# Average pooling over 671 MB: every transfer issued by GpSimd on one queue, each as one packet per DMA engine

## The chip, the cores and the metric

The kernel runs on one core of a Trainium2 chip. The metric is the device time of one execution in microseconds (us); a kernel's time is the median of several runs. A transfer between the chip's memory (HBM) and the core's on-chip memory of 128 partitions is carried by 16 DMA engines; an engine of the core issues it, and the kernel's instructions wait for its completion by a semaphore.

## The reference

Means over windows of four neighbours, without overlap, of a float32 array of 64 x 256 x 8192 (536.87 MB in, 134.22 MB out):

```python
def reference(x, kernel_size, stride):          # 4 and 4
    batch, channels, length = x.shape           # 64, 256, 8192
    out_len = (length - kernel_size) // stride + 1
    output = np.zeros((batch, channels, out_len), dtype=np.float32)
    for i in range(out_len):
        start = i * stride
        output[:, :, i] = np.mean(x[:, :, start : start + kernel_size], axis=2)
    return output
```

## The kernel before

The array is seen as 16384 rows of 8192 numbers. `_packed_fast_path` (the path that this shape takes) cuts them into 32 groups of 512 rows; a partition holds four neighbouring rows of a group, f = 0 to 3. So a group is four input tiles `xt` of 128 x 8192 (4 MiB each, 32 KiB in each partition) and one output tile `ot` of 128 x 8192 (also 4 MiB).

For each tile the loop does three things: SyncE (SP) issues the load (L245); VectorE (DVE) adds the four neighbours with one `tensor_reduce` into a quarter of `ot` (L246); ScalarE (ACT) multiplies that quarter by 1/4 in place (L252). After the fourth tile, ACT issues the store of the whole group (L253). There are three buffers for `xt` and two for `ot`; a load into a buffer waits for the reduce that read it last. SP's queue thus holds the loads, ACT's queue the stores, and both queues run on the same 16 DMA engines.

The last group is cut finer, so that little is left to do after the last byte has arrived: its second and third tile are loaded and reduced in thirds (L263, L266), its fourth in six pieces of falling size (L284, L293), 1668, 2268, 1632, 1172, 844 and 608 columns. The first three tiles' results of this group (6144 columns) are stored by SP in four equal parts, issued behind the last piece's load (L292). The results of the first five pieces are stored by ACT, one by one (L310); the last piece is scaled by VectorE into a tile of its own, `fin` (L300), and stored by SP (L307).

On SP the order is: loads of all tiles, the four parts of the last group's store, the last piece's store. On ACT: four scalings, one store, and so on. GpSimd (POOL) only sets four constants.

Of the kernel before, what the change touches and what calls it, by code (L numbers as in the profile page):

```python
# [7 lines left out]
_N_PARK = 4  # L8
_FINAL_COLS_TGT = 608
_LADDER_RATIO = 1.39  # L10
_NCHUNK_PRE = 3
_PACK_STORES = True
_PACK_F_MAX = 4


def _tail_ladder(total: int, k: int, final: int, ratio: float = _LADDER_RATIO,
                 max_chunks: int = 12) -> list:
    if total < 4 * final:
        return [total]
    rev = []  # L20
    s = 0
    w = float(final)
    while len(rev) < max_chunks - 1:
        wi = max(k, (int(round(w)) // k) * k)
        if s + wi > total - k:
            break
        rev.append(wi)
        s += wi
        w *= ratio
    sizes = [total - s] + rev[::-1]  # L30
    assert sum(sizes) == total and all(x > 0 and x % k == 0 for x in sizes)
    return sizes


def _even_chunks(total: int, k: int, n: int) -> list:
    n = max(1, min(n, total // k))
    q = (total // n) // k * k
    sizes = [q] * n
    sizes[-1] += total - q * n
    assert sum(sizes) == total and all(s > 0 and s % k == 0 for s in sizes)  # L40
    return sizes


@with_exitstack
def kernel(
    ctx: ExitStack,
    tc: tile.TileContext,
    x: bass.AP,
    kernel_size: bass.AP,
    stride: bass.AP,  # L50
    out: bass.AP,
):
    nc = tc.nc

    K = int(kernel_size)
    S = int(stride)
    assert K == S, "only stride == kernel_size supported"

    B, C, L = x.shape
    OL = (L - K) // S + 1  # L60
    assert OL * K <= L

    P = nc.NUM_PARTITIONS

    xf = x.flatten_outer_dims()
    of = out.flatten_outer_dims()
    rows = B * C

    inv_k = 1.0 / float(K)
    dt = x.dtype  # L70
    IL = OL * K

    if _PACK_STORES and IL == L:
        F = 0
        for cand in range(_PACK_F_MAX, 1, -1):
            if rows % (P * cand) == 0 and (rows // (P * cand)) >= 2:
                F = cand
                break
        if F >= 2 and L >= 64 * K and OL % 8 == 0 and OL * F * 4 <= 32768:
            _packed_fast_path(nc, tc, xf, of, rows, L, OL, K, F, inv_k, dt, P)  # L80
            return

    RPP = 1
    R = P * RPP
    NT = rows // R
    IL2 = RPP * L
    OL2 = RPP * OL
    fast = (
        IL == L
        and rows % R == 0  # L90
        and NT >= 6
        and IL2 >= 64 * K
        and OL % 2 == 0
    )

    if not fast:
        with (
            tc.tile_pool(name="xin", bufs=4) as pin,
            tc.tile_pool(name="res", bufs=4) as pout,
        ):  # L100
            r0 = 0
            while r0 < rows:
                rn = min(P, rows - r0)
                xt = pin.tile([P, IL], dt)
                ot = pout.tile([P, OL], dt)
                nc.sync.dma_start(out=xt[:rn], in_=xf[r0 : r0 + rn, :IL])
                nc.vector.tensor_reduce(
                    out=ot[:rn],
                    in_=xt[:rn].rearrange("p (m k) -> p m k", k=K),
                    axis=mybir.AxisListType.X,  # L110
                    op=mybir.AluOpType.add,
                )
                nc.scalar.mul(ot[:rn], ot[:rn], inv_k)
                nc.scalar.dma_start(out=of[r0 : r0 + rn], in_=ot[:rn])
                r0 += P
        return

    def xview(t):
        return xf[t * R : (t + 1) * R]

    def oview(t):
        return of[t * R : (t + 1) * R]

    ladder = _tail_ladder(IL2, K, _FINAL_COLS_TGT)
    chunks_pre = _even_chunks(IL2, K, _NCHUNK_PRE)
    fin_w = ladder[-1] // K

    with (
        tc.tile_pool(name="xin", bufs=4) as pin,
        tc.tile_pool(name="res", bufs=4) as pout,  # L130
        tc.tile_pool(name="rsv", bufs=1) as prsv,
        tc.tile_pool(name="fin", bufs=1) as pfin,
    ):
        rsv = prsv.tile([P, OL2], dt)
        fin = pfin.tile([P, fin_w], dt)

        for t in range(NT):
            xv = xview(t)
            ov = oview(t)
            xt = pin.tile([P, IL2], dt)  # L140
            ot = rsv if t == 0 else pout.tile([P, OL2], dt)

            if t == 0:
                nc.sync.dma_start(out=xt[:, :IL2], in_=xv[:, :IL2])
                nc.vector.tensor_reduce(
                    out=ot[:, :OL2],
                    in_=xt[:, :IL2].rearrange("p (m k) -> p m k", k=K),
                    axis=mybir.AxisListType.X,
                    op=mybir.AluOpType.add,
                )  # L150
                nc.scalar.mul(ot[:, :OL2], ot[:, :OL2], inv_k)
            elif t < NT - 3:
                nc.sync.dma_start(out=xt[:, :IL2], in_=xv[:, :IL2])
                nc.vector.tensor_reduce(
                    out=ot[:, :OL2],
                    in_=xt[:, :IL2].rearrange("p (m k) -> p m k", k=K),
                    axis=mybir.AxisListType.X,
                    op=mybir.AluOpType.add,
                )
                nc.scalar.mul(ot[:, :OL2], ot[:, :OL2], inv_k)  # L160
                nc.scalar.dma_start(out=ov[:, :OL2], in_=ot[:, :OL2])
            elif t < NT - 1:
                c0 = 0
                for cw in chunks_pre:
                    c1 = c0 + cw
                    o0, o1 = c0 // K, c1 // K
                    nc.sync.dma_start(out=xt[:, c0:c1], in_=xv[:, c0:c1])
                    nc.vector.tensor_reduce(
                        out=ot[:, o0:o1],
                        in_=xt[:, c0:c1].rearrange("p (m k) -> p m k", k=K),  # L170
                        axis=mybir.AxisListType.X,
                        op=mybir.AluOpType.add,
                    )
                    nc.scalar.mul(ot[:, o0:o1], ot[:, o0:o1], inv_k)
                    nc.scalar.dma_start(out=ov[:, o0:o1], in_=ot[:, o0:o1])
                    c0 = c1
            else:
                nchunk = len(ladder)
                c0 = 0
                for i, cw in enumerate(ladder):  # L180
                    c1 = c0 + cw
                    o0, o1 = c0 // K, c1 // K
                    last = i == nchunk - 1
                    nc.sync.dma_start(out=xt[:, c0:c1], in_=xv[:, c0:c1])
                    if last:
                        q0 = 0
                        qw = (OL2 - q0) // _N_PARK
                        for qi in range(_N_PARK):
                            qa = q0 + qi * qw
                            qb = q0 + (qi + 1) * qw if qi != _N_PARK - 1 else OL2  # L190
                            nc.sync.dma_start(
                                out=oview(0)[:, qa:qb], in_=rsv[:, qa:qb]
                            )
                    nc.vector.tensor_reduce(
                        out=ot[:, o0:o1],
                        in_=xt[:, c0:c1].rearrange("p (m k) -> p m k", k=K),
                        axis=mybir.AxisListType.X,
                        op=mybir.AluOpType.add,
                    )
                    if last:  # L200
                        nc.vector.tensor_scalar(
                            out=fin[:, :fin_w],
                            in0=ot[:, o0:o1],
                            scalar1=inv_k,
                            scalar2=None,
                            op0=mybir.AluOpType.mult,
                        )
                        nc.sync.dma_start(out=ov[:, o0:o1], in_=fin[:, :fin_w])
                    else:
                        nc.scalar.mul(ot[:, o0:o1], ot[:, o0:o1], inv_k)  # L210
                        nc.scalar.dma_start(out=ov[:, o0:o1], in_=ot[:, o0:o1])
                    c0 = c1


def _packed_fast_path(nc, tc, xf, of, rows, L, OL, K, F, inv_k, dt, P):
    R = P * F
    NTM = rows // R

# [10 lines left out]
    with (  # L229
# [6 lines left out]
        for t in range(NTM):  # L236
            xv = xe(t)
# [109 lines left out]
```

## Time and profile before

| | |
|---|---|
| median of 3 runs | 1561.14 us (1561.12 to 1561.38) |
| profiled execution, first to last instruction | 1559.04 us |
| bytes read from HBM and written to it | 536.87 MB, 134.22 MB |
| mean rate over the span | 430 GB/s |
| one reduce of a whole tile (VectorE, L246) | 8686 ns, 124 of them |
| one scaling of 128 x 2048 (ScalarE, L252) | 1911 ns, 124 of them |
| one issue of a load by SP / of a store by ACT | 328 ns / 338 ns |
| a load's time from issue to landing, median | 26.4 us |
| a group store's time from issue to landing, median | 23.2 us |

How to read it: the span is one execution as the hardware profiler saw it. "Busy" counts only work of the engine itself; issuing a transfer does not count. A transfer's data move as packets on the 16 DMA engines; a packet record has a start, a duration, a size and a queue. Of a table by stretches of time the columns are: the stretch, its length, then busy time and number of instructions of VectorE, ScalarE and GpSimd, the clock granted to the (unused) TensorE, the mean busy share of the 16 DMA engines, and the bytes moved per time. The share can exceed 1 a little, since neighbouring packets of an engine overlap in the records.

### The profile page before, as it was taken

To read this page: it belongs to the slowest core of one execution; us is meant where nothing else is said; L and a number is where in the kernel's file an instruction comes from. 1 tells how busy PE (TensorE), PEld (TensorE's weight loads), DVE (VectorE), ACT (ScalarE), POOL (GpSimd) and SP (SyncE) were. 2 spreads that over 40 slices of the span, in tenths; PEclk is the share of its full clock that TensorE was granted. 3 is DMA by queue.
4 is the path that set the end of the run, shared out by engine and by line. 5 is a ranking of instruction groups with operands and counts; after the bars stand their busy time and mean duration, and the time that the engine had idled before them with its cause. 6 is when DMAs were issued, how large, how long until landed. Compare 5 with 4: busy or idle time off the path is not lost.

```text
span 1559.0 us, 724 instructions
## 1 busy us (share of the span) xinstructions
DVE 1112.8 (71%) x138; ACT 247.4 (16%) x137; POOL 0.2 (0%) x4
## 2 busy tenths in 40 slices
DVE  6777667776667866677666776667766677766786
ACT  1111111111111111111111111111111111111111
POOL 0000000000000000000000000000000000000000
DMA  9999999999999999999999999999999999999999
GB/s 416 418 430 436 437 432 430 430 430 432 439 433 430 430 432 430 438 434 431 430 432 430 435 434 433 431 431 430 433 437 433 432 430 431 430 437 434 432 427 384
DMA packets 25637, 671.14 MB, mean 430 GB/s; under 512 B 2848, under 2 KB 3488, under 8 KB 4768
## 3 DMA queue, kind: packets, MB, share of 16 engines
q1 hardware_dynamic: 20448, 540.10, 80.6%
q10 hardware_dynamic: 5184, 131.00, 19.5%
q14 instruction: 5, 0.04, 0.0%
HBM read 536.87 MB, written 134.22 MB: 430 GB/s over the span
## 4 chain that ended last, share of the span: by engine, by line
DMA 75%; DVE 24%; issue 0%; SPq 0%; DVEq 0%
DMA xt<-in_x_dram 75%; DVE ot L246 23%; DVE ot L293 1%; DVE ot L266 0%; SPq L263 0%; DVEq L246 0%; DVE fin L300 0%
## 5 line engine op out<-in xcount | busy, mean ns | idle before, releaser
L246 DVE TENSOR_REDUCE ot<-xt 128x2048 f32<-128x8192 f32 x124 | 1077.1, 8686 | 430.2 <-DMA xt<-in_x_dram 430.2
L252 ACT ACTIVATE ot<-ot 128x2048 f32<-128x2048 f32 x124 | 237.0, 1911 | 1270.2 <-DVE ot L246 1270.2
L266 DVE TENSOR_REDUCE ot<-xt 128x682 f32<-128x2728 f32 (+2 forms) x7 | 26.6, 3809 | 6.9 <-DMA xt<-in_x_dram 6.9
L272 ACT ACTIVATE ot<-ot 128x682 f32<-128x682 f32 (+2 forms) x7 | 6.6, 936 | 25.8 <-DVE ot L266 25.8
L293 DVE TENSOR_REDUCE ot<-xt 128x417 f32<-128x1668 f32 (+5 forms) x6 | 9.0, 1568 | 0.0
L309 ACT ACTIVATE ot<-ot 128x417 f32<-128x417 f32 (+4 forms) x5 | 2.6, 521 | 5.2 <-DVE ot L293 5.2
L252 ACT ACT_TABLE_LOAD x1 | 1.3, 1283 | 0.7 <-PEq L328 0.7
L300 DVE TENSOR_SCALAR fin<-ot 128x152 f32<-128x152 f32 x1 | 0.2, 239 | 0.0
L328 POOL MEMSET const-bfloat16-1.0<- 128x1 bf16 x1 | 0.1, 102 | 0.0
L328 POOL MEMSET const-uint8-127<- 128x1 uint8 x1 | 0.1, 102 | 0.0
L328 POOL MEMSET const-float32-0.0<- 128x1 f32 x1 | 0.1, 99 | 0.2 <-issue 0.2
L328 POOL MEMSET const-float32-1.0<- 128x1 f32 x1 | 0.1, 99 | 0.0
## 6 DMA issues: line engine op xcount, KB each, us to landing
xt<-in_x_dram SPq DMA_DIRECT2D x125, 4096.0 KB, 26.4
out_dram<-ot ACTq DMA_DIRECT2D x31, 4096.0 KB, 23.2
xt<-in_x_dram SPq DMA_DIRECT2D x4, 1364.0 KB, 23.4
out_dram<-ot SPq DMA_DIRECT2D x4, 768.0 KB, 7.7
xt<-in_x_dram SPq DMA_DIRECT2D x2, 1368.0 KB, 29.5
xt<-in_x_dram SPq DMA_DIRECT2D x1, 1134.0 KB, 16.2
xt<-in_x_dram SPq DMA_DIRECT2D x1, 834.0 KB, 22.6
xt<-in_x_dram SPq DMA_DIRECT2D x1, 816.0 KB, 17.8
```

The source lines that it names most:

```text
L246: nc.vector.tensor_reduce(out=ot[:, o0 : o0 + OL], in_=xt[:, :L].rearrange("p (m k) -> p m k", k=K), axis=mybir.AxisListType.X, op=mybir.A ...
L252: nc.scalar.mul(ot[:, o0 : o0 + OL], ot[:, o0 : o0 + OL], inv_k)
L266: nc.vector.tensor_reduce(out=ot[:, o0:o1], in_=xt[:, c0:c1].rearrange("p (m k) -> p m k", k=K), axis=mybir.AxisListType.X, op=mybir.AluOp ...
L272: nc.scalar.mul(ot[:, o0:o1], ot[:, o0:o1], inv_k)
L293: nc.vector.tensor_reduce(out=ot[:, o0:o1], in_=xt[:, c0:c1].rearrange("p (m k) -> p m k", k=K), axis=mybir.AxisListType.X, op=mybir.AluOp ...
L300: nc.vector.tensor_scalar(out=fin[:, :fin_w], in0=ot[:, o0:o1], scalar1=inv_k, scalar2=None, op0=mybir.AluOpType.mult,)
L309: nc.scalar.mul(ot[:, o0:o1], ot[:, o0:o1], inv_k)
L328: nc = _bacc.Bacc("TRN2", target_bir_lowering=False, num_devices=1)
```

## The change

The kernel is written anew around the same tiling: 32 groups, four tiles each, the same thirds and the same six pieces at the end. What differs:

- Every transfer, load and store, is issued by GpSimd (`dma = nc.gpsimd`), whose descriptors are written by software, and all stand in one queue in program order. SP and ACT issue none.
- Every transfer carries `single_packet=True`: each engine's share of a transfer is one packet.
- There are four buffers for `xt` in place of three.
- A group's store isn't issued after its last scaling, but behind the second load of the next group (`AHEAD = 2`).
- The end: all six pieces' loads, then the four parts of the store of the first three tiles (`PARK = 4`), then one store for the first four pieces and one for the last two. The last two pieces are scaled by VectorE in place; `fin` is gone.

```diff
-        tc.tile_pool(name="xin", bufs=3) as pin,
-        tc.tile_pool(name="res", bufs=2) as pout,
-        tc.tile_pool(name="fin", bufs=1) as pfin,
...
-                    nc.sync.dma_start(out=xt[:, :L], in_=xv[:, f * L : (f + 1) * L])
...
-                nc.scalar.dma_start(out=ov[:, : F * OL], in_=ot[:, : F * OL])
...
+    dma = nc.gpsimd
...
+    pin = ctx.enter_context(tc.tile_pool(name="xin", bufs=4))
+    pout = ctx.enter_context(tc.tile_pool(name="res", bufs=2))
+
+    def load(g, xt, f, a, b):
+        dma.dma_start(out=xt[:, a:b], in_=xg(g)[:, f * L + a : f * L + b], single_packet=True)
+
+    def means(xt, ot, f, a, b, scale_on_dve=False):
+        o = ot[:, f * OL + a // K : f * OL + b // K]
+        nc.vector.tensor_reduce(
+            out=o,
+            in_=xt[:, a:b].rearrange("p (m k) -> p m k", k=K),
+            axis=mybir.AxisListType.X,
+            op=mybir.AluOpType.add,
+        )
+        if scale_on_dve:
+            nc.vector.tensor_scalar(
+                out=o, in0=o, scalar1=1.0 / K, scalar2=None, op0=mybir.AluOpType.mult
+            )
+        else:
+            nc.scalar.mul(o, o, 1.0 / K)
+
+    def store(g, ot, a, b):
+        dma.dma_start(out=og(g)[:, a:b], in_=ot[:, a:b], single_packet=True)
+
+    held = None
+    for g in range(groups):
+        ot = pout.tile([P, F * OL], dt, name="ot")
+        for f in range(F):
+            xt = pin.tile([P, L], dt, name="xt")
+            if (g, f) == (groups - 1, F - 1):
+                break
+            cuts = THIRDS if g == groups - 1 and f > 0 else (L,)
+            edges = [sum(cuts[:i]) for i in range(len(cuts) + 1)]
+            for a, b in zip(edges[:-1], edges[1:]):
+                load(g, xt, f, a, b)
+            if held is not None and f == AHEAD - 1:
+                store(*held, 0, F * OL)
+            for a, b in zip(edges[:-1], edges[1:]):
+                means(xt, ot, f, a, b)
+        held = g, ot
+
+    f = F - 1
+    edges = [sum(LADDER[:i]) for i in range(len(LADDER) + 1)]
+    n = len(LADDER) - 2
+    for a, b in zip(edges[:-1], edges[1:]):
+        load(g, xt, f, a, b)
+    for i in range(PARK):
+        store(g, ot, i * f * OL // PARK, (i + 1) * f * OL // PARK)
+    for a, b in zip(edges[:n], edges[1 : n + 1]):
+        means(xt, ot, f, a, b)
+    store(g, ot, f * OL, f * OL + edges[n] // K)
+    for a, b in zip(edges[n:-1], edges[n + 1 :]):
+        means(xt, ot, f, a, b, scale_on_dve=True)
+    store(g, ot, f * OL + edges[n] // K, F * OL)
```

More of the change, by code (lines that the diff above doesn't have):

```diff
@@ L6 @@
 from concourse._compat import with_exitstack
[L8 to L41, printed above, removed]
+F = 4
+AHEAD = 2
+LADDER = (1668, 2268, 1632, 1172, 844, 608)
+THIRDS = (2728, 2728, 2736)
+PARK = 4
 @with_exitstack
@@ L53 @@
     nc = tc.nc
-    K = int(kernel_size)
-    S = int(stride)
-    assert K == S, "only stride == kernel_size supported"
+    K, S = int(kernel_size), int(stride)
+    assert K == S == 4
     B, C, L = x.shape
-    OL = (L - K) // S + 1
-    assert OL * K <= L
+    OL = L // K
     P = nc.NUM_PARTITIONS
+    dt = x.dtype
+    dma = nc.gpsimd
     xf = x.flatten_outer_dims()
     of = out.flatten_outer_dims()
[L67 to L77, printed above, removed]
-                break
-        if F >= 2 and L >= 64 * K and OL % 8 == 0 and OL * F * 4 <= 32768:
-            _packed_fast_path(nc, tc, xf, of, rows, L, OL, K, F, inv_k, dt, P)
-            return
@@ L83 @@
[L83 to L131, printed above, removed]
-        tc.tile_pool(name="fin", bufs=1) as pfin,
[L133 to L212, printed above, removed]
@@ L215, in _packed_fast_path @@
-def _packed_fast_path(nc, tc, xf, of, rows, L, OL, K, F, inv_k, dt, P):
-    R = P * F
-    NTM = rows // R
-    ladder = _tail_ladder(L, K, _FINAL_COLS_TGT)
-    chunks_pre = _even_chunks(L, K, _NCHUNK_PRE)
-    fin_w = ladder[-1] // K
-    def xe(t):
-        return xf[t * R : (t + 1) * R].rearrange("(p f) m -> p (f m)", f=F)
-    def oe(t):
-        return of[t * R : (t + 1) * R].rearrange("(p f) m -> p (f m)", f=F)
-    with (
-        tc.tile_pool(name="xin", bufs=3) as pin,
-        tc.tile_pool(name="res", bufs=2) as pout,
-        tc.tile_pool(name="fin", bufs=1) as pfin,
-    ):
-        fin = pfin.tile([P, fin_w], dt)
-        for t in range(NTM):
-            xv = xe(t)
-            ov = oe(t)
-            ot = pout.tile([P, F * OL], dt)
-            if t < NTM - 1:
-                for f in range(F):
-                    xt = pin.tile([P, L], dt)
-                    o0 = f * OL
-                    nc.sync.dma_start(out=xt[:, :L], in_=xv[:, f * L : (f + 1) * L])
-                    nc.vector.tensor_reduce(
-                        out=ot[:, o0 : o0 + OL],
-                        in_=xt[:, :L].rearrange("p (m k) -> p m k", k=K),
-                        axis=mybir.AxisListType.X,
-                        op=mybir.AluOpType.add,
-                    )
-                    nc.scalar.mul(ot[:, o0 : o0 + OL], ot[:, o0 : o0 + OL], inv_k)
-                nc.scalar.dma_start(out=ov[:, : F * OL], in_=ot[:, : F * OL])
-                continue
-            for f in range(F - 1):
-                xt = pin.tile([P, L], dt)
-                widths = [L] if f < F - 3 else chunks_pre
-                c0 = 0
-                for cw in widths:
-                    c1 = c0 + cw
-                    o0, o1 = f * OL + c0 // K, f * OL + c1 // K
-                    nc.sync.dma_start(
-                        out=xt[:, c0:c1], in_=xv[:, f * L + c0 : f * L + c1]
-                    )
-                    nc.vector.tensor_reduce(
-                        out=ot[:, o0:o1],
-                        in_=xt[:, c0:c1].rearrange("p (m k) -> p m k", k=K),
-                        axis=mybir.AxisListType.X,
-                        op=mybir.AluOpType.add,
-                    )
-                    nc.scalar.mul(ot[:, o0:o1], ot[:, o0:o1], inv_k)
-                    c0 = c1
-            fq = F - 1
-            xt = pin.tile([P, L], dt)
-            hold = fq * OL
-            nchunk = len(ladder)
-            c0 = 0
-            for i, cw in enumerate(ladder):
-                c1 = c0 + cw
-                o0, o1 = fq * OL + c0 // K, fq * OL + c1 // K
-                last = i == nchunk - 1
-                nc.sync.dma_start(
-                    out=xt[:, c0:c1], in_=xv[:, fq * L + c0 : fq * L + c1]
-                )
-                if last:
-                    qw = hold // _N_PARK
-                    for qi in range(_N_PARK):
-                        qa = qi * qw
-                        qb = (qi + 1) * qw if qi != _N_PARK - 1 else hold
-                        nc.sync.dma_start(out=ov[:, qa:qb], in_=ot[:, qa:qb])
-                nc.vector.tensor_reduce(
-                    out=ot[:, o0:o1],
-                    in_=xt[:, c0:c1].rearrange("p (m k) -> p m k", k=K),
-                    axis=mybir.AxisListType.X,
-                    op=mybir.AluOpType.add,
-                )
-                if last:
-                    nc.vector.tensor_scalar(
-                        out=fin[:, :fin_w],
-                        in0=ot[:, o0:o1],
-                        scalar1=inv_k,
-                        scalar2=None,
-                        op0=mybir.AluOpType.mult,
-                    )
-                    nc.sync.dma_start(out=ov[:, o0:o1], in_=fin[:, :fin_w])
-                else:
-                    nc.scalar.mul(ot[:, o0:o1], ot[:, o0:o1], inv_k)
-                    nc.scalar.dma_start(out=ov[:, o0:o1], in_=ot[:, o0:o1])
-                c0 = c1
@@ new lines, with xg, og @@
+    R = P * F
+    groups = B * C // R
+    assert B * C == groups * R
+    assert sum(LADDER) == sum(THIRDS) == L
+    def xg(g):
+        return xf[g * R : (g + 1) * R].rearrange("(p f) m -> p (f m)", f=F)
+    def og(g):
+        return of[g * R : (g + 1) * R].rearrange("(p f) m -> p (f m)", f=F)
+    pin = ctx.enter_context(tc.tile_pool(name="xin", bufs=4))
+    pout = ctx.enter_context(tc.tile_pool(name="res", bufs=2))
+    def load(g, xt, f, a, b):
+        dma.dma_start(out=xt[:, a:b], in_=xg(g)[:, f * L + a : f * L + b], single_packet=True)
```

## The prediction

> **What bounds the kernel now.** I read the page first, busy times, slices and queues; then the chain that ended last; then the answer by stretches of time; then the timeline of the end; last the trace's records of single packets.
>
> ```profile
> span 1559.0 us, 724 instructions
> DVE 1112.8 (71%) x138; ACT 247.4 (16%) x137; POOL 0.2 (0%) x4
> ...
> DMA packets 25637, 671.14 MB, mean 430 GB/s; under 512 B 2848, under 2 KB 3488, under 8 KB 4768
> q1 hardware_dynamic: 20448, 540.10, 80.6%
> q10 hardware_dynamic: 5184, 131.00, 19.5%
> ...
> DMA xt<-in_x_dram 75%; DVE ot L246 23%; DVE ot L293 1%; DVE ot L266 0%; SPq L263 0%; DVEq L246 0%; DVE fin L300 0%
> ```
>
> VectorE is busy for 71%, ScalarE for 16%, GpSimd for nothing. The two queues (q1 of SP, q10 of ACT) together hold the 16 DMA engines for 80.6 + 19.5 = 100.1% of the span. So the chain's 23% on L246 misleads: it goes through VectorE because a load waits for a buffer, but the DMA engines never lack work meanwhile. The stretches say so:
>
> ```profile
> 20.00:40.00 20.00, 17.97 (x3) 3.82 (x2) 0.00 (x0) 1.00 1.00 433
> ...
> 886.31:1031.76 145.45, 104.23 (x12) 22.93 (x12) 0.00 (x0) 1.00 1.00 433
> ...
> 1540.00:1550.00 10.00, 9.91 (x8) 3.38 (x6) 0.00 (x0) 1.00 1.02 413
> 1550.00:1559.00 9.00, 0.00 (x0) 0.00 (x0) 0.00 (x0) 1.00 0.68 268
> ```
>
> The last two columns are DMA share and GB/s. From 886.31 to 1031.76 us the chain passes exactly three groups (four loads and one store of 4 MiB each), 145.45 / 3 = 48.48 us a group, and the share is 1.00. The time is thus bytes over the engines' rate, plus a head and a tail. A change pays if it makes an engine spend less than 48.48 us on its 1,310,720 bytes of a group, or if it shortens the ends.
>
> **What an engine's time is made of.** The packet records have one packet for each 32 KiB row and one of 4 bytes for each completion: (128 + 16) x 142 transfers = 20448, q1's number. Median durations: 4 B 9 ns, 608 B 31 ns, 6144 B 234 ns, 32768 B 1213 ns. The slope of the last two is 979 / 26624 = 0.03677 ns a byte, so the bytes of a 32 KiB packet take 1204.9 ns, and about 8 ns are the packet's own, as for the packet of 4 bytes. A group's bytes need 1,310,720 x 0.03677 = 48.20 us; 48.48 - 48.20 = 0.28 us is overhead, 6.3 ns for each of its 45 packets (less than 8, since neighbours overlap).
>
> **The change, part by part.** *One packet for each engine and transfer.* Of a group's 45 packets an engine keeps 5. If all that overhead goes with the boundaries, 32 groups win 32 x 0.28 = 9 us; if it belongs to each row's descriptor, nothing is won. No row shows a packet of several rows. I take a part: large packets average 3.1 ns over their median, half of it in 52 stretched ones, so some 1.6 of the 6.3 ns is scatter that no boundary makes. The nearest row, the 4-byte packet, costs its 9 ns with next to no data, which speaks for the packet as the cause. So 4.7 ns x 40 x 32 = **-6.0 us** (0 to -9).
>
> The Trainium skill has a rule against this part. In "DMA: Bandwidth & Descriptors", section "Why small descriptors are slow (HBM only)", it gives a fixed overhead of about 3 cycles for a packet and holds that joining descriptors is only worth it up to 256 bytes each. With the 850 MHz of its section "Where 436 GB/s comes from" that would be an estimate of 3.5 ns x 40 x 32 = -4.5 us, and by its verdict on large descriptors 0.
>
> *Stores.* 174 transfers in place of 178: the end has two stores for its last 2048 columns, not six. 4 x 9 packets x 6.3 ns = -0.2 us.
>
> *The start.* Before, SP issues at 0.73 us and the first packet starts at 1.73 us. Now GpSimd writes the descriptors. No row has that; the bounds are 0 and the cost of code being loaded as in ACT_TABLE_LOAD, 1.28 us, taken twice, 2.6. I take +1.0. At 54 us, when the first store joins, ten packets of about 2 us stand in the records; the 5 us stretches from 50 and 55 us are about 16 and 68 GB/s short of 433, together 1.0 us. One queue and a fourth buffer may remove that: 0 to -1.0, taken -0.5.
>
> *One queue in order.* A store now stands between loads. Let a group's last load land at T. Its reduce takes 8.69 us and its scaling 1.91, so the store issues at T + 10.7. Behind it on GpSimd wait the third and fourth load of the next group, and VectorE waits for them. Ahead of it are two loads, 2 x 9.7 = 19.4 us of DMA work. The cover is 8.7 us, so nothing is lost; if it were gone, each us beyond it would cost 1 us in each of 31 groups. Loads wait for the reduce of the tile four before, which ends 8.7 us after that tile lands, with three loads still queued. A group's output buffer returns one group before it is wanted. Cost 0. The 31 store issues leave ACT (338 ns each, under 84% idle time) and 137 load issues leave SP: 0. GpSimd had four memsets, and 174 issues at any price below 1559 / 174 = 8.9 us fit.
>
> L246 takes 8686 ns for 8192 inputs, 1.06 ns each; if GpSimd could write no descriptor while a reduce runs, the store would be put off to the end of the reduce then running, T + 18.4, still inside 19.4, so even that costs about 0. A second rule of the Trainium skill is the reason to ask: "SBUF — State Buffer", section "SBUF: two separate sides", warns that VectorE in a two-port mode locks GpSimd out of writing descriptors. "VectorE: DVE Perf Modes" lists this reduce with a 1x form only, so by the pages no lock is due.
>
> *The tail.*
>
> ```profile
> 1540.65 9.02 DVE L293 TENSOR_REDUCE ot<-xt 128x417 f32<-128x1668 f32 x6
> ...
> 1549.71 0.24 DVE L300 TENSOR_SCALAR fin<-ot 128x152 f32<-128x152 f32 x1
> ...
> 1552.79 0.38 SPq L307 DMA_DIRECT2D out_dram<-fin x1
> ```
>
> The last store issues 2.8 us after its data are ready, yet packets run until 1556, the last one to 1557.6. The 1.6 us of ramp there is the most to win. After, 4 MiB of stores, 9.7 us, stand behind the last load, while reduce, two scalings and an issue need about 3 us: hidden. A slower GpSimd issue may cost as much: -1.5 to +1.5, taken 0.
>
> Sum: -6.0 - 0.2 + 1.0 - 0.5 + 0 = **-5.7 us**, on the span of 1559.04: 1553.3. The runs' median, 1561.14, lies 2.1 us above that span (work outside the first and last instruction); kept, this gives **1555.4 us**.
>
> **Rivals.** *A, the forecast*: the overhead belongs to packet boundaries. For it: 9 ns for 4 bytes. Against: a boundary and a descriptor are the same thing in every row.
>
> *B, nothing is joined, or joining doesn't pay*: the overhead is each row's. Then the sum is -0.2 + 1.0 - 0.5 = +0.3, 1561.4 us. For it: a large packet is within 0.7% of its pure bytes. It is also the case that the change doesn't do what it says.
>
> *C, slower: a gap at the head of each transfer on the one software-written queue*. The place is the hand-over from one transfer to the next on each engine: with one queue no other has packets ready to fill it. Price: g x 174. Against it, from 20 to 40 us only loads run, on one queue, at share 1.00: hardware-written transfers follow without a gap, so the lower bound is 0. The other bound is the 0.33 us that SP's issuing instruction takes for one transfer, if that were spent at every hand-over: 57 us, 1613. It decides from 5.7 / 174 = 33 ns on. Between ends so far apart I place C at 0.08 us, a quarter of the upper, since the one queue's row is near 0: +14 us, 1569.
>
> **How the numbers follow.** About 0.2% (3.1 us) is what a measurement can tell from no change: 1558.0 to 1564.3 is the same. A 0.57, B 0.18, C 0.25. Of A 0.53 is faster and 0.04 the same (a small packet gain with a dear start); of B 0.03, 0.11 and 0.04 are faster, same and slower; of C 0.01 is the same and 0.24 slower. Faster 0.56, same 0.16, slower 0.28. The low end takes A's bounds: -9 - 0.2 - 1.0 = -10.2 and half of the tail's gain, 1550. The high end is C's placed value, 1569; about half of C lies beyond, 0.12, and some 0.04 below the low end. A's own range is 1550 to 1559.
>
> **What would show it.** A: packets fall from 25637 towards a fifth or less or, if the records still list rows, these take less than 1213 ns; the group's period falls below 48.4 us, the middle slices rise from 433 to 434 to 435 GB/s. B: the period stays at 48.48. C: the share in the middle falls below 1.00, with idle stretches as often as there are transfers. Start: the first reduce, at 12.74 us before, comes about 1 us later. One queue: GpSimd's waits for ScalarE must not leave the DMA share under 1.00 in mid-group. The prediction falls if the rate of single packets changes (more than 0.03677 ns a byte), or if the first load lands many us late.

## The result, and the profile after

The changed kernel takes 1566.20 us (median of 6 runs, 1565.48 to 1566.45) against 1561.13 us before (6 runs, 1560.99 to 1561.40): slower by 5.07 us, ratio 1.0032 with a 95% interval of 1.0023 to 1.0042. The forecast was 1555.4 us, faster. The profiled execution took 1565.48 us, with a span of 1563.56 us.

The page of the changed kernel, its busy times, packet count and queue, then the chain that ended last:

```profile
span 1563.6 us, 685 instructions
DVE 1112.7 (71%) x139; ACT 246.8 (16%) x136; POOL 91.9 (6%) x178
...
DMA packets 24852, 671.13 MB, mean 429 GB/s; under 512 B 2784, under 2 KB 2784, under 8 KB 3984
q0 software_dynamic: 24848, 671.10, 99.8%
...
DMA xt<-in_x_dram 81%; DVE ot L58 17%; POOL xt L54 0%; POOLq L135 0%; POOL out_dram L72 0%; POOLq L72 0%; PEldq L135 0%
```

One queue, q0, carries everything, as the change says. But there are 24852 packets, not a fifth of 25637: hardly any were joined. That a transfer goes as one packet for each engine, as the title and the list of changes have it, isn't what the records show. The DMA engines are still the bound (99.8%). GpSimd spends 92 us on issuing, 6% of the span.

The stretches of the changed kernel, with the same columns as before:

```profile
886.31:1031.76 145.45, 104.16 (x13) 22.91 (x12) 7.89 (x15) 1.00 1.00 432
...
1550.00:1563.00 13.00, 2.47 (x5) 0.45 (x1) 1.07 (x2) 1.00 0.59 247
```

In the middle the share is 1.00, as before, and the rate hardly differs. So most of the 5 us must be sought at the two ends.

The start, from the timeline of the kernel before:

```profile
0.73 75.33 SPq L245 DMA_DIRECT2D xt<-in_x_dram  x9
12.74 8.69 DVE L246 TENSOR_REDUCE ot<-xt 128x2048 f32<-128x8192 f32 x1 [12.74 <-DMA xt<-in_x_dram]
```

and of the changed kernel:

```profile
1.27 2.23 POOL L54 DMA_DIRECT2D xt<-in_x_dram  x4 [0.83 <-PEq L135]
13.62 8.69 DVE L58 TENSOR_REDUCE ot<-xt 128x2048 f32<-128x8192 f32 x1 [13.62 <-DMA xt<-in_x_dram]
```

GpSimd issues the first load at 1.27 us (SP did at 0.73), and the first reduce starts at 13.62 us (before: 12.74). The packet records say the same: first packet at 2.64 us, before at 1.73.

The end is best seen in the sequencers' own instructions, here those of the changed kernel's closing line (L135), each with count, shortest, median and longest duration in ns and the first and last start in us:

```profile
L135 POOLq EVENT_SEMAPHORE  x4: 17/17/17, 1562.9 to 1563.5; - x4
L135 POOLq DRAIN  x3: 40/89/10109, 1552.7 to 1563.3; - x3
L135 SPq DRAIN  x3: 7/7/7, 1560.2 to 1563.1; - x3
```

and the same of the kernel before (L342):

```profile
L342 POOLq EVENT_SEMAPHORE  x4: 17/17/17, 1558.4 to 1558.9; - x4
L342 POOLq DRAIN  x3: 34/41/70, 0.7 to 1558.8; - x3
L342 SPq DRAIN  x3: 7/7/7, 1558.3 to 1558.6; - x3
```

Before, SP sees the last transfer landed at 1558.3 us, and GpSimd answers at 1558.4; its DRAINs take 70 ns at most. After, SP is as far at 1560.2 us, but GpSimd answers at 1562.9: one DRAIN of it (an instruction that ends only when what its engine has issued is done, by the runs below) started at 1552.74 and took 10.109 us, until 1562.85, while the last transfer had landed at 1560.03. The program's end waits 2.8 us for an instruction that cost nothing before.

Packet records (count and mean duration in ns, by size in bytes, taken from the trace itself):

```
size          before                  after
32768         median 1213             median 1213     (19968 of them in both)
rows of 2432  128 x 98.8              64 x 191.1      as 4864: two rows in one
rows of 1452  -                       16 x 115.4, 32 x 169.9   as 2904, 4356: two and three rows in one
rows of 3376  128 x 134.9             64 x 264.9      as 6752: two rows in one
rows of 4688  128 x 182.0             128 x 182.0     single
```

So rows are joined after all, but only until a packet holds some 4 KiB or more; a row of 4688 bytes or more stays alone. The kernel's rows are nearly all of 32 KiB.

### The profile page after: what moved, and what is told of

The parts are those of the page before. It is cut to its first block, busy times and chain, and to the rows that moved or that the text cites. A ratio compares the mean times of both kernels' runs of the same rounds, so it can differ in the third digit from the quotient of the medians.

```text
span 1563.6 us, 685 instructions
## 1 busy us (share of the span) xinstructions
DVE 1112.7 (71%) x139; ACT 246.8 (16%) x136; POOL 91.9 (6%) x178
## 2 busy tenths in 40 slices
DMA packets 24852, 671.13 MB, mean 429 GB/s; under 512 B 2784, under 2 KB 2784, under 8 KB 3984
## 3 DMA queue, kind: packets, MB, share of 16 engines
q0 software_dynamic: 24848, 671.10, 99.8%
## 4 chain that ended last, share of the span: by engine, by line
DMA 81%; DVE 17%; issue 1%; POOL 0%; POOLq 0%; PEldq 0%
DMA xt<-in_x_dram 81%; DVE ot L58 17%; POOL xt L54 0%; POOLq L135 0%; POOL out_dram L72 0%; POOLq L72 0%; PEldq L135 0%
## 5 line engine op out<-in xcount | busy, mean ns | idle before, releaser
L58 DVE TENSOR_REDUCE ot<-xt 128x2048 f32<-128x8192 f32 (+3 forms) x137 | 1112.4, 8125 | 439.8 <-DMA xt<-in_x_dram 439.8
L69 ACT ACTIVATE ot<-ot 128x2048 f32<-128x2048 f32 (+2 forms) x135 | 245.5, 1819 | 1303.4 <-DVE ot L58 1303.4
L54 POOL DMA_DIRECT2D xt<-in_x_dram x137 | 72.1, 529 | 510.4 <-DVE ot L58 489.9
L72 POOL DMA_DIRECT2D out_dram<-ot x37 | 19.8, 536 | 950.8 <-ACT ot L69 946.2
```

What stands on the lines that cost most here:

```text
L54: dma.dma_start(out=xt[:, a:b], in_=xg(g)[:, f * L + a : f * L + b], single_packet=True)
L58: nc.vector.tensor_reduce(out=o, in_=xt[:, a:b].rearrange("p (m k) -> p m k", k=K), axis=mybir.AxisListType.X, op=mybir.AluOpType.add,)
L69: nc.scalar.mul(o, o, 1.0 / K)
L72: dma.dma_start(out=og(g)[:, a:b], in_=ot[:, a:b], single_packet=True)
```

## The experiments

The suspects were: the flag; the two ends of the software queue; the single queue; the fourth buffer. All times are medians; the kernel before was timed beside each lot and stayed between 1561.01 and 1561.08 us.

### Without the flag

```diff
-        dma.dma_start(out=xt[:, a:b], in_=xg(g)[:, f * L + a : f * L + b], single_packet=True)
+        dma.dma_start(out=xt[:, a:b], in_=xg(g)[:, f * L + a : f * L + b])
...
-        dma.dma_start(out=og(g)[:, a:b], in_=ot[:, a:b], single_packet=True)
+        dma.dma_start(out=og(g)[:, a:b], in_=ot[:, a:b])
```

> The changed kernel without the one-packet flag; all else as it is. Theory 1 (the flag joins nothing, since each row of 32 KiB is a packet of its own in the records of both kernels): the time stays at 1566 us within 1 us, the packet records keep their sizes and counts (19968 of 32768 bytes, median 1213 ns). Rival (the flag gains some of the 6 us that I forecast, and something else of the software queue loses 11): 1570 to 1573 us, and more or longer packets.

1566.0 us (ratio to before 1.0032, 1.0019 to 1.0045), as with the flag. The page's packet lines of this kernel are those of the changed one to the packet:

```profile
DMA packets 24852, 671.13 MB, mean 429 GB/s; under 512 B 2784, under 2 KB 2784, under 8 KB 3984
q0 software_dynamic: 24848, 671.10, 99.7%
```

The flag does nothing here. The joining of short rows happens with and without it.

### All on SyncE, one queue

```diff
-    dma = nc.gpsimd
+    dma = nc.sync
```

(and without the flag)

> The changed kernel with every transfer issued by SyncE in place of GpSimd, in the same order on one queue, without the flag. Theory 1 (the loss is the software queue's two ends: first packet 0.9 us later, GpSimd's DRAIN ending 2.8 us after the last landing, some 2.5 us more than before): about 1562 us, first packet near 1.7 us after the start, about 1.4 us from the last packet to the end. Rival (the loss is that of one queue in order, or of the fourth buffer, or of the later store): it stays at 1566 us.

1562.37 us (1.0008, 0.9999 to 1.0017): 3.8 us of the 5.07 go with the software queue. The first packet is at 1.75 us. GpSimd's DRAIN is short again, by the sequencers' instructions of this kernel:

```profile
L135 POOLq DRAIN  x3: 34/41/70, 0.7 to 1561.0; - x3
```

Some 1.3 us over the kernel before remain, on one hardware queue, though the interval just reaches 1.

### The last group by SyncE

```diff
     def load(g, xt, f, a, b):
-        dma.dma_start(out=xt[:, a:b], ..., single_packet=True)
+        if g == groups - 1:
+            nc.sync.dma_start(out=xt[:, a:b], ...)
+        else:
+            dma.dma_start(out=xt[:, a:b], ..., single_packet=True)
```

and the same in `store`.

> The changed kernel with all transfers of the last group (its loads and its stores) issued by SyncE; everything else stays with GpSimd, the first loads too. GpSimd's DRAIN then has more than 40 us in which to end. Theory 1 (the DRAIN's time after the last landing is on the path): 2.4 to 2.8 us under the changed kernel, 1563.3 to 1563.8 us. Rival (something else at the end, as SyncE's waits or the landing of the last stores): 1565.5 us or more.

1563.19 us (1.0014, 1.0005 to 1.0023), 3.0 us under the changed kernel. The long DRAIN is still there, but it starts at 1532.0 us and ends at 1549.6, before the last landing, and hides:

```profile
L141 POOLq DRAIN  x3: 45/101/17651, 1532.0 to 1561.3; - x3
```

The last landing is no earlier than in the changed kernel, 1560.32 us against 1560.03, so it is the end behind it that has shrunk: from the last landing to the last instruction 1.21 us, not 3.54 (0.92 in the kernel before). The time is 0.8 us over the run on SyncE alone, about the 0.9 us by which the first packet is later.

### Both ends by SyncE: a trial that went astray

As the last, with the first group's loads by SyncE too.

> The changed kernel with the first group's loads and all transfers of the last group (loads and stores) issued by SyncE; the 30 groups between stay with GpSimd. Theory 1 (the loss lies at the two ends): 3 to 3.5 us under the changed kernel, about 1562.5 to 1563 us, and GpSimd's DRAIN ends before the last landing. Rival (the loss is spread over the stream, as by slower packets or an engine that lags): at most 0.5 us less, 1565.5 us or more.

1573.89 us (1.0083, 1.0069 to 1.0096), far over all expectations. The stretches of this kernel show why:

```profile
50.00:60.00 10.00, 0.96 (x1) 0.24 (x1) 0.00 (x0) 1.00 0.99 426
60.00:70.00 10.00, 10.00 (x2) 1.91 (x1) 0.04 (x1) 1.00 0.00 0
70.00:80.00 10.00, 10.00 (x2) 1.91 (x1) 2.07 (x4) 1.00 1.08 419
```

From 60 to 70 us nothing moves. GpSimd's first loads shared the engines with SyncE's third and fourth, so these landed late, at 39.6 and 59 us; next on GpSimd's queue stood the first group's store, which waits for the scaling of the tile that landed at 59 us, and behind it the loads. In the records no packet runs for 10.1 us. It tells nothing of the ends, but it is the wait that the prediction costed at nothing, with its cover gone.

### What the DRAIN depends on

Three kernels leave the kernel before as it is but for some transfers by GpSimd; a fourth is the changed kernel with its loads on SyncE.

```diff
-                    nc.sync.dma_start(out=ov[:, o0:o1], in_=fin[:, :fin_w])
+                    nc.gpsimd.dma_start(out=ov[:, o0:o1], in_=fin[:, :fin_w])
```

> The kernel before, with its very last store (76 KB, from fin) alone issued by GpSimd. If the DRAIN at the end has a fixed price once GpSimd has issued a transfer: about 1.5 to 3 us more than before, 1563 to 1564 us, with the DRAIN ending some 2.8 us after the last landing. If its price grows with the number of transfers issued on the software queue (174 in the changed kernel): less than 0.5 us, 1561.1 to 1561.6 us.

1561.14 us (1.0001, 0.9992 to 1.0009), no cost: the DRAIN ended 0.08 us after its transfer's landing, and other stores were later.

```profile
L342 POOLq DRAIN  x3: 34/88/5631, 1550.3 to 1558.9; - x3
```

With the last group's ten stores by GpSimd (L292, L307 and L310 so changed; tried after the two below):

> The kernel before with the last group's ten stores, and nothing else, issued by GpSimd. The DRAIN ended 2.8 us after the last landing with 174 transfers issued by GpSimd, 1.56 with 37, 1.37 with 138, 0.08 with 1: not in step with their number. If its price goes with the transfers still in flight when it starts (half a dozen stores in the changed kernel): 1.5 to 3 us here. If it goes, however loosely, with all that GpSimd has issued: 0.1 to 0.6 us.

1562.27 us (1.0008, 0.9998 to 1.0017); the DRAIN ended at 1559.64 us, 0.45 us after the last landing.

```profile
L342 POOLq DRAIN  x3: 34/101/2345, 1557.3 to 1560.1; - x3
```

The 1.2 us, between the two expectations, are not the DRAIN's alone: the last landing is at 1559.19 us in place of 1558.12. The first of these stores is now issued at 1519.4 us, not at 1539.8, and they run beside the last loads, the last of which lands at 1555.7 us, not at 1548.1.

The changed kernel with `nc.sync` in `load`, 37 stores left to GpSimd:

> The changed kernel with all loads issued by SyncE and the 37 stores left to GpSimd, with the flag. If the DRAIN at the end costs some 16 ns for each transfer that GpSimd has issued (0.08 us after the last landing with 1, 2.8 us with 174), it ends about 0.7 us after the last landing here, and with first packets at 1.75 us and two queues the time is 1561.5 to 1562.5 us. Rival (the price is fixed as soon as GpSimd has issued many or the last ones): 2.5 us or more after the last landing, 1563.5 to 1564.5 us.

1564.25 us (1.0020, 1.0012 to 1.0029); 1.56 us after the last landing, not 0.7, nor 2.5.

```profile
L135 POOLq DRAIN  x3: 40/101/4441, 1556.9 to 1561.9; - x3
```

Here the last stores also land 1.7 us later than before's (1559.81 against 1558.12 us): the last load lands at 1555.1 us, and from 1554 to 1556 us the engines hardly move anything while the last results are made.

The kernel before with all loads and the last store by GpSimd, group stores left to ScalarE:

```diff
-                    nc.sync.dma_start(out=xt[:, :L], in_=xv[:, f * L : (f + 1) * L])
+                    nc.gpsimd.dma_start(out=xt[:, :L], in_=xv[:, f * L : (f + 1) * L])
```

(and so at L263, L284 and L307)

> The kernel before with all 137 loads and the very last store issued by GpSimd without the flag, the group stores left to ScalarE: software descriptors, but two queues. From the parts: start +0.9 us, the DRAIN ending some 2 us later after the last landing than before's end (138 transfers; 0.08 us with 1, 1.56 with 37, 2.82 with 174), no loss in the stream (packets at 1215.0 ns): 1563.5 to 1564.3 us. Rival (software descriptors slow the stream): packets at 1216 ns or more, and 1565 us or more.

1563.69 us (1.0018, 1.0009 to 1.0027); 1.37 us after the last landing, with a first packet at 2.64 us.

```profile
L342 POOLq DRAIN  x3: 40/101/3256, 1558.7 to 1562.5; - x3
```

The time is as expected, but partly by luck: the DRAIN costs less than the 2 us put in, and the last loads again land late (1557.1 us).

The traces of two runs shown above belong beside these: their DRAINs ended before the program's end, but also some time after the landing of GpSimd's own last transfer. With all seven:

```
transfers issued by GpSimd              1     10    37    138   151   155   174
DRAIN ends after their last landing, us 0.08  0.45  1.56  1.37  1.89  2.04  2.82
```

(151 is the run with both ends by SyncE, 155 that with the last group by SyncE; 174 is the changed kernel, with or without the flag.) The time isn't fixed. Nor does it go with the number in flight when the DRAIN begins, which was 3 with ten transfers, 2 with 37, and 1 with 155. It does grow with the number issued: from 1 to 37 each further transfer adds 41 ns, from 138 to 174 each adds 40 ns. But the second stretch starts lower, as if some 105 of the transfers no longer counted. No run lies between 37 and 138, so where and why the count starts over stays open.

### The 1.3 us of the single queue

First the fourth buffer by itself:

```diff
-        tc.tile_pool(name="xin", bufs=3) as pin,
+        tc.tile_pool(name="xin", bufs=4) as pin,
```

> The kernel before with four input buffers in place of three, nothing else. If the 16 DMA engines never lack work (share 1.00 in the middle), a buffer more changes nothing: 1561.1 us within 0.5. Rival (the fourth buffer is part of what one queue costs, since a load that is issued earlier runs without a store beside it): about 1562 us.

1561.10 us (1.0000, 0.9992 to 1.0009): nothing.

Then the changed kernel's tiling, order and buffers on two hardware queues (`nc.sync` in `load`; in `store` `nc.scalar`, for the last group `nc.sync`):

> The changed kernel's tiling, order and four buffers with all loads issued by SyncE and the group stores by ScalarE (the last group's stores by SyncE). If one queue costs 1.3 us because loads then never run beside a store (in the middle of the span large packets take 1216.2 ns on the mean with all on SyncE, 1215.0 ns before, where loads beside a store take 1213.8): back to 1561.1 us, packets at 1215.0. Rival (the 1.3 us is from the rewritten end or the later store): it stays at 1562.3 us.

1560.59 us (0.9998, 0.9989 to 1.0006), 1.8 us under the run with all on SyncE. Mean durations of 32 KiB packets from 100 to 1480 us, in the records:

```
one queue    changed 1215.8   without flag 1216.2   all on SyncE 1216.2   last group by SyncE 1215.9
two queues   before 1215.0    four buffers 1215.0   SyncE + ScalarE 1215.0
             loads by GpSimd 1215.0                 stores by GpSimd 1215.0
```

The dividing line is the number of queues, not who writes the descriptors. An engine carries 1248 such packets, so 0.8 to 1.2 ns are 1.0 to 1.5 us. The times alone would not carry this: the intervals of both runs, 0.9999 to 1.0017 on one hardware queue and 0.9989 to 1.0006 on two, reach 1. The packet records do.

They also show that the reason given in the expectation is the smaller part. On two queues 4 or 5 of the 32 KiB packets from 100 to 1480 us take over 1250 ns; on one queue 54 do in the changed kernel, 118 with all on SyncE, and 59 to 148 in the other three. What they take beyond 1213 ns comes to 0.74 us on each engine in the changed kernel and 1.33 with all on SyncE, against 0.12 in the kernel before, which is most of the difference. They stand where the one queue turns from loads to a store or back: 50 of the 54, and 95 of the 118, start in the 5 us ahead of the landing at such a turn, and none ahead of the 105 landings between two loads. The remaining 0.2 to 0.3 us fit the expectation's reason: from a store's first packet to its last, loads take 1213.4 ns on the mean in the kernel before, otherwise 1215.9, and on one queue no load runs then. Why packets at a turn are stretched was not tried.

### Fewer packets by longer rows

If the overhead belongs to the packet, it can be saved by longer rows instead. First rows of 64 KiB, two tiles to a load, with two buffers of that size:

```diff
-        tc.tile_pool(name="xin", bufs=3) as pin,
+        tc.tile_pool(name="xin", bufs=2) as pin,
...
-                for f in range(F):
-                    xt = pin.tile([P, L], dt)
+                for f in range(0, F, 2):
+                    xt = pin.tile([P, 2 * L], dt, name="xt")
...
-                    nc.sync.dma_start(out=xt[:, :L], in_=xv[:, f * L : (f + 1) * L])
+                    nc.sync.dma_start(out=xt[:, :], in_=xv[:, f * L : (f + 2) * L])
...
```

> The kernel before with loads of two tiles at once (64 KiB in each partition, two buffers of that size) in all groups but the last; stores as they were. If an engine's overhead of 6.3 ns belongs to each packet and a row of 64 KiB is one packet: 31 x 16 packets fewer on each engine, 3.1 us less, about 1558 us. If such a row is cut into two packets, or the overhead goes with the bytes: 1561.1 us. If two buffers starve the engines: more, with a DMA share under 1.00 in the middle.

1616.59 us (1.0357, 1.0343 to 1.0371). A row of 64 KiB is one packet with a median of 2418 ns, 8 ns less than two of 1213. But 938 of the 7936 took over 2700 ns, 3135 at the median, which makes 43 us on each engine, of the 55.5 us lost. They are the first packets, about two on each engine, of every second load. Such a load was issued only 3.2 us (median) before the load ahead of it had landed, the others 12.3 us; so the queue was about to run dry. The engines count as busy meanwhile, so the share says nothing of it:

```profile
886.31:1031.76 145.45, 98.47 (x13) 22.91 (x12) 0.00 (x0) 1.00 0.99 415
```

Share 0.99 and yet 415 GB/s. Then three loads to a group, with three buffers:

```diff
-                for f in range(F):
-                    xt = pin.tile([P, L], dt)
+                for cw in (10924, 10920, 10924):
+                    xt = pin.tile([P, 10924], dt, name="xt")
...
```

> The kernel before with three loads of 10924, 10920 and 10924 columns for a group (rows of 43.7 KB) in place of four of 8192, three buffers of that size. If 6 to 8 ns belong to each packet: 31 x 8 packets fewer on each engine, 1.5 to 2.0 us less, 1559.1 to 1559.6 us, with the engines fed as before since two loads are always queued. If the overhead goes with the bytes: 1561.1 us.

1558.76 us (0.9986, 0.9977 to 0.9995), 2.25 us under the kernel before and 7.4 under the changed one: the fastest of all. The page and the chain of waits of this kernel:

```profile
DMA packets 21172, 671.13 MB, mean 431 GB/s; under 512 B 2352, under 2 KB 2992, under 8 KB 4272
```

```profile
914.97 11.54 DVE ot L247
...
963.40 11.54 DVE ot L247
...
1011.83 11.54 DVE ot L247
```

4465 packets fewer (31 x 9 x 16 = 4464, completions included), and a period of 48.43 us a group against 48.48 (over 27 groups, from landing to landing, 48.44 against 48.53). An engine has 31 x 9 = 279 packets fewer; 2.25 us for them are 8 ns each, a little more than was expected. The interval of the ratio allows 3 to 13 ns.

## Why the prediction was wrong

*What bounds the kernel*: right for the middle. The share was 1.00 there before and after, and no engine's work came onto the path. At the end GpSimd's DRAIN did.

*What an engine's time is made of*: right in kind, a little small in size. The overhead does belong to packets: fewer of them gained 2.25 us, 8 ns a packet where the prediction had 6.3; two rows of 2432 bytes in one packet take 191 ns, not 2 x 98.8. Part of the difference is that the three groups from which the prediction took its period run short: over 27 groups it is 48.53 us, not 48.48, which makes the prediction's own sum 7.4 ns.

*One packet for each engine and transfer, -6.0 us*: this step failed, and with it the sign. The measured value is 0 (1566.2 us with the flag, 1566.0 without). The prediction assumed that 40 of 45 packets would go, and weighed only whether the boundary or the row carries the cost. The records show that rows of 32 KiB are not joined at all, with or without the flag. It was named as rival B ("nothing is joined"), at 0.18, and only one sentence weighed it; that the records of before have a packet for each row on the hardware queues said nothing of the software one, and the middle value between 0 and -9 rested on no row of a joined packet. The rule of the Trainium skill that the prediction quoted from "DMA: Bandwidth & Descriptors", section "Why small descriptors are slow (HBM only)", by which joining large descriptors isn't worth it, pointed the right way here, though for another reason: the overhead that joining would save is there (8 ns a packet), only rows this long aren't joined.

*Stores, -0.2*: too small to be told apart. *The start, +1.0*: right in size, 0.91 us from the first packets, but by luck, since the value was picked between 0 and 2.6; 0.54 us of it is that GpSimd issues later. *The 54 us event, -0.5*: not gained; by the packet records the 5 us stretches from 55 and 60 us run at 414 and 364 GB/s in the changed kernel, much as those from 50 and 55 us did before (417 and 365).

*One queue in order, 0*: the step on the waits holds, for the share stays at 1.00; the trial with both ends on SyncE shows the wait once its cover is gone. GpSimd's 137 issues of loads took 527 to 667 ns, with reduces of 8.69 us running, so no reduce held one up. But the step had another price, which it put at nothing: packets stretched where the one queue turns between loads and a store. The changed kernel's program costs 1562.37 us on one hardware queue and 1560.59 on two; against the kernel before it is +1.3 us.

*The tail, 0, from -1.5 to +1.5*: wrong in mechanism. The DMA work was hidden as argued. What ended the program was GpSimd's DRAIN, 2.8 us after the last landing; moving the last group to SyncE takes 3.0 us away, and in its trace the last landing is not earlier. The row stood in the trace of before, at 70 ns, and I read the closing line's instructions only after the result. An instruction that waits for what its engine has issued costs nothing on an engine that issues nothing.

*The sum*: the spans of the two profiled executions, 1559.04 and 1563.56 us, are 4.53 us apart. The first packet comes 0.91 us later; from it to the last landing the changed kernel takes 1.00 us longer, the stream on one queue; from there to the last instruction 2.62 us longer (3.54 against 0.92), the DRAIN. That is all of the 4.53. The medians are 5.07 us apart; the profiled execution of the changed kernel was the fastest of its six, and no trace shows the other 0.5 us.

*The rivals*: B described the stream (its 1561.4 us has neither the queue nor the DRAIN). C had the right sign, but not its mechanism: the share in the middle stays at 1.00, nothing is seen at the hand-overs from load to load, and GpSimd's issue, 527 ns a load, is hidden by up to three queued loads. Only at the turns between loads and stores are packets stretched, for 0.6 us an engine more than before, where C had 14 us. The stated range held the time; the direction was wrong.

## What to carry to other kernels

On a stream that keeps the DMA engines full, count the packets in the records before costing anything that is to join them, and look at what decides a packet's size (here some 4 KiB, or one row where that is longer); longer rows did what the flag didn't, as long as the next load was issued well ahead. When an engine begins to issue transfers, read the closing instructions of the program too: the end of its queue becomes part of the time. Loads and stores on two queues were worth about a microsecond here, though the one queue never ran dry.

## What was not expected of the hardware

- Software-written descriptors join short rows in one packet, flag or not: two rows of 2432 bytes took 191.1 ns, three of 1452 bytes 169.9 ns; on the hardware queue of the run with all on SyncE single rows of 2432 and 1452 bytes took 98.8 and 62.0 ns. The packet is closed at about 4 KiB: in the run with the last ten stores by GpSimd six rows of 608 bytes (3648) took a seventh, five of 844 bytes (4220) no sixth.
- GpSimd's DRAIN went on for 0.08 to 2.82 us after the landing of its last transfer, some 41 ns for each transfer issued, with a step down between 37 and 138.
- A busy share of 0.99 can hide a queue that is about to run dry: first packets of 3135 ns in place of 2418 where the load was issued 3.2 us before the one ahead had landed.
- On one queue packets are stretched where loads give way to a store or come back: 54 to 148 of over 1250 ns in the middle of the span, against 4 or 5 on two queues.
